# Four gates as two more pairs of seven products, with less fill per retention chunk

## The chip, the core and the metric

The kernel runs on one core of a Trainium2 chip. A core has five engines that work side by side, each on its own queue of instructions: TensorE (PE, matmuls; its weight loads are listed as PEld), VectorE (DVE), ScalarE (ACT), GpSimd (POOL) and SyncE (SP, which here issues most of the DMA loads). POOL issues the stores. Matmul results land in PSUM, in banks of 128 x 512 floats, and DVE and ACT take them from there. The metric is the time of one execution on the device, in microseconds (us); the time given for a kernel is the median of its runs.

## The reference

One layer of an encoder in float32: a half-step feed-forward part, a token mixing, and a second half-step feed-forward part, each between two RMS norms. The sequence has 1024 tokens of width 1024. The change lies in the token mixing:

```python
def _token_mixing(u, w_in, ..., w_ret_out, w_na_out, w_out, pos):
    rq, rk, rv, rg, nq, nk, nv, g_ret, g_na = jnp.split(u @ w_in, points, axis=-1)
    ...
    y = _bidirectional_retention(q, k, heads(rv, RET_V_DIM), decay_fwd, decay_bwd)
    y = y * lax.rsqrt(jnp.mean(y * y, axis=-1, keepdims=True) + RMS_EPS)
    ...
    y_ret = (jax.nn.silu(rg) * y) @ w_ret_out
    y_na = _neighborhood_attention(na_heads(nq), na_heads(nk), na_heads(nv), rel_bias) @ w_na_out
    merged = jax.nn.sigmoid(g_ret) * y_ret + jax.nn.sigmoid(g_na) * y_na
    return merged @ w_out
```

One projection of u gives everything: queries, keys, values and a Silu gate for the retention (4 heads, 128 wide keys, 256 wide values), queries, keys and values for the neighbourhood attention (8 heads of 64), and two gates as wide as the model, `g_ret` and `g_na`. The retention runs over chunks of 128 tokens in both directions. `sigmoid(g_na)` is what the change is about: 1024 columns, eight blocks of 128.

## The kernel before

**Precision.** Every operand is split into a high and a low part (`split`, lines 57 to 66: ACT copies the high part with rounding, DVE subtracts it from the source), and every product is three matmuls, high x high, high x low, low x high (`mm3`, lines 92 to 96).

**Pairs of seven products.** A projection block can be computed in two ways. Directly, as in `gate` (line 1475), one block of 128 output columns over 1024 tokens is 2 halves of the tokens times 8 steps of 128 input columns, each a `mm3` of three 128 x 512 matmuls. Or two blocks together as a `Pairs.run` (line 555), a Winograd form of Strassen's scheme: weights and activations are cut into quarters, and seven products of 4 steps each (12 matmuls) take the place of eight. The activations' factors (a11, a12, a22, s1 to s4) are in SBUF already; the weights' factors are made per pair by DVE, and DVE also adds up the results out of PSUM. The list `jobs` (lines 1400 to 1404) says which blocks go as pairs: four of the neighbourhood's queries and keys, then alternating a pair of the retention's queries and keys (with rotary) and a pair of its Silu gate, and at last two pairs of `g_na`, blocks 0 to 3. Pairs 3, 12 and 13 have their first two products computed earlier, by `leads` at line 1409, and read them back. The loop at line 1434 runs the pairs one after the other; `run` prepares the next pair's weights on the way unless it is told not to (`nxt`, false for pair 3 and the last). What isn't in `jobs` is computed directly.

**Fill.** The neighbourhood attention (`na_cores`, line 929) and the retention (`ret_cores`, line 1120) are made of small matmuls with long chains through DVE and ACT. So that PE has something to do meanwhile, `products` (line 1490) is a generator of independent work, one `mm3` per step, and the two functions call `fill(n)` at fixed places to issue n steps of it. The steps come in a fixed order: 128 for the retention's values (`vproj`) and one that only marks their end, four `g_na` gates (blocks 4 to 7) of 16 steps, four `g_ret` gates of 16, four halves of 8, four halves of 8 with a split of the attention's output between them, and 64 for the neighbourhood's output projection, which multiplies by the `g_na` gates read back from memory (line 1512). That is 385. `NA_FILL` (12, 2, 2) gives 12 steps ahead of the neighbourhood attention and 2 + 2 in each of its 34 rounds, 148 in all. `RET_FILL` has nine numbers, used in `ret_cores` as n[0] to n[8]: ahead of everything (line 1222), at a head's begin (1226), after each of the 7 updates of the backward sweep (1233), before the scores (1239), before the forward chunks (1242), in each of the 8 chunks between the scores and the update (1248), behind the chunk's products (1266), behind the store (1269), and ahead of each store that is left at the very end (1272). What is left of the fill then is drained at line 1536.

**A retention head.** The backward sweep (line 1231) updates the backward state chunk by chunk: three 128 x 256 matmuls (`update`), whose results DVE accumulates (line 1174, tile `sb`). The forward part (line 1243) has, per chunk, the scores of the next chunk, an update of the forward state `st` with its split into `sfh` and `sfl`, the products `cross` (with both states) and `inner`, and a norm, whose result is transposed on PE and multiplied by the Silu gate (`rg`, line 1217) one or two chunks later. In the last chunk the keys of the next head are transposed, scaled and split (`kdec`, tiles `kdh`, `kdl`), and the next head's k, q and v are split (`kl`, `ql`, `vl`). Behind the last head stands the retention's output projection: the gated result is loaded again and split (tile `xy`, line 1545) and multiplied.

**Order.** A planner places the instructions of each engine at build time, by the program's order and by when it reckons their operands ready. Each engine then runs its queue in that order.

Of the kernel before, what the change touches and what calls it, by code (L numbers as in the profile page):

```python
# [13 lines left out]
AF = mybir.ActivationFunctionType  # L14
# [14 lines left out]
NHP = 4  # L29

NA_FILL = (12, 2, 2)
RET_FILL = (14, 2, 2, 4, 2, 3, 0, 1, 2)
FLIP_FILL = (12, 12, 12, 12, 2)
LOADS = (6, 9, 12, 15, 18, 22, 28, 33, 38)
NA_UNITS = ((0, 0, 0), (3, 1, 0), (1, 0, 1), (1, 0, 2), (4, 1, 1), (4, 1, 2), (2, 0, 3), (5, 1, 3))
# [1241 lines left out]
def trunk_layer(ctx: ExitStack, tc, x, xt, g1a, w1i, w1o, g1b, gma, wmt, wnv, wrv, logits, dtab, rope, bias,  # L1277
# [11 lines left out]
    def dt(name, shape):  # L1289
        return dram.tile(shape, F32, name=name)  # L1290
# [3 lines left out]
    d = {  # L1294
        "a21": dt("a21", [P, 4, 512]),
        "nq": dt("nq", [NHP, P, S]), "nk": dt("nk", [NHP, P, S]), "nv": dt("nv", [16, 64, 512]), "nvg": dt("nvg", [4, 4, P, 512]),
        "no": dt("no", [NHP, P, S]), "rq": dt("rq", [RH, P, S]), "rk": dt("rk", [RH, P, S]),
        "rv": dt("rv", [TT, P, D]), "rg": dt("rg", [8, P, S]), "ry": dt("ry", [8, P, S]),
        "dec": dt("dec", [P, 536]), "far": dt("far", [3, 2, P, 512]), "far1": dt("far1", [3, 2, P, 512]), "far2": dt("far2", [3, 2, P, 512]), "sr": dt("sr", [8, P, S]), "sn": dt("sn", [8, P, S]), "z": dt("z", [8, P, S]), "m": dt("m", [8, 2, P, S]),
    }  # L1300
# [6 lines left out]
    def pool(stack, name, side="left"):  # L1307
        return stack.enter_context(tc.tile_pool(name=name, bufs=1, side=side, reuse_waits="tile"))
# [46 lines left out]
    def xh(t, k):  # L1355

        return a21 if (t, k) == (1, 0) else wx.op(("a11", "a12", None, "a22")[2 * t + k])
# [3 lines left out]
    def vproj(src, groups, done):  # L1361

        w = []
        for toks in groups:
            banks = {t: c.bank() for t in toks}
            for k in range(KT):
                if k == len(w):
                    w += ahead.pop(k // 2) if k // 2 in ahead else c.load_w(src[k // 2])
                    if k > 3 and qk:
                        c.after(c.fetch, qk)  # L1370
                        qk.clear()
                for t in toks:
                    tt = slice((t % 4) * P, (t % 4 + 1) * P)
                    c.mm3(banks[t], [q[:, k % 4, tt] for q in xh(t // 4, k // 4)], w[k], k == 0, k == KT - 1)
                    yield
            for t in toks:
                done(t, banks[t])
# [3 lines left out]
    def ev():  # L1381
        return evpool[0].tile([P, S], F32, tag="ev", name="ev", bufs=3)
# [9 lines left out]
    def done_rv(j):  # L1392
        def f(t, b):
            e = ev()
            nc.scalar.copy(e[:, :512], b)
            c.store(d["rv"][t][:, j * 512:(j + 1) * 512], e[:, :512])
        return f


    jobs = [(16 + i, 20 + i, d["nq"][i], d["nk"][i], None) for i in range(NHP)]  # L1400
    for i in range(RH):
        jobs += [(i, 4 + i, d["rq"][i], d["rk"][i], "rotary"),
                 (8 + 2 * i, 9 + 2 * i, d["rg"][2 * i], d["rg"][2 * i + 1], AF.Silu)]
    jobs += [(32 + 2 * i, 33 + 2 * i, d["sn"][2 * i], d["sn"][2 * i + 1], AF.Sigmoid) for i in range(2)]
    mx = Pairs(c, wx, [(wmt[j[0]], wmt[j[1]]) for j in jobs], 3, joined=False)

    def first():
# [67 lines left out]
    def gate(i, dst, halves=(0, 1)):  # L1475

        w = c.load_w(wmt[i])
        e = ev()
        for h in halves:
            hs = slice(h * 512, (h + 1) * 512)  # L1480
            b = c.bank()
            for k in range(KT):
                ks = slice((k % 4) * P, (k % 4 + 1) * P)
                c.mm3(b, [p[:, ks] for p in w[k // 4]], [q[:, k % 4] for q in xh(h, k // 4)], k == 0, k == KT - 1)
                yield
            nc.scalar.activation(e[:, hs], b, AF.Sigmoid)
        hs = slice(halves[0] * 512, halves[-1] * 512 + 512)
        c.store(dst[:, hs], e[:, hs])

    def products():  # L1490
        for j in range(2):
            yield from vproj(wrv[j], ((0, 1, 2), (3, 4, 5), (6, 7)), done_rv(j))
        yield "rv"
        for i in range(4, 8):
            yield from gate(32 + i, d["sn"][i])
        for i in range(4):
            yield from gate(24 + i, d["sr"][i])
        for i in range(4, 8):
            yield from gate(24 + i, d["sr"][i], (1,))
        x1_stack.close()  # L1500
        opool = pool(o_stack, "o", "right")
        oop = [opool.tile([P, 4, S], F32R, name=f"o{q}") for q in "hl"]
        for i in range(4, 8):
            raw = c.raw(d["no"][i - 4])
            c.split(oop[0][:, i - 4], oop[1][:, i - 4], raw)
            yield from gate(24 + i, d["sr"][i], (0,))

        for i in range(8):
            if i % 2 == 0:
                w = c.load_w(wno[i // 2])  # L1510
            e = ev()
            nc.sync.dma_start(e, d["sn"][i])
            for h in range(2):
                hs = slice(h * 512, (h + 1) * 512)
                b = c.bank()
                for k in range(4):
                    c.mm3(b, [p[:, k * P:(k + 1) * P] for p in w[i % 2]], [q[:, k, hs] for q in oop], k == 0, k == 3)
                    yield
                nc.vector.tensor_tensor(e[:, hs], b, e[:, hs], ALU.mult)
            c.store(d["z"][i], e)  # L1520

    fill = Filler(products())
    with tc.tile_pool(name="na", bufs=1, reuse_waits="tile") as na:
        early = []
# [5 lines left out]
    with tc.tile_pool(name="ret", bufs=1, reuse_waits="tile") as ret:  # L1530
        ret_cores(c, ret, mix, d, dec, fill, RET_FILL, early)
    y_stack = ExitStack()
# [175 lines left out]
```

## Time and profile before

| what | us |
|---|---|
| median of 3 runs | 2209.81 |
| lowest and highest run | 2209.61 and 2209.9 |
| the profiled execution, its time | 2210.64 |
| its span, first to last instruction | 2208.9 |
| PE busy in the span | 2186.8 |
| DVE busy | 1574.1 |
| ACT busy | 959.9 |
| POOL busy | 588.7 |

The profile's page is of one execution. An engine's busy time is the union of its instructions' durations; matmuls overlap in it. The granted clock of TensorE was 0.999 of full speed. In the trace the pairs of the mixing run from about 700 to 975 us, the neighbourhood attention from about 975 to 1150, the retention from about 1155 to 1390. L94, L95 and L96 are the three matmuls of `mm3`, L62 and L63 the two instructions of `split`. A name such as `wl<-wraw,wh` is the tile written and the tiles read.

### The profile page before, as it was taken

What the parts mean: (1) busy time and instruction counts of PE and PEld (TensorE: products, weight loads), DVE (VectorE), ACT (ScalarE), POOL (GpSimd) and SP (SyncE); (2) the same over time, 40 slices, a digit from 0 to 9 for tenths busy, and PEclk for the clock granted to TensorE, in tenths of its full rate; (3) what the DMA queues carried; (4) which work ended last, traced back from release to release, by engine and by line L of the source; (5) the groups of instructions that cost most, each with busy time, mean ns of one, the idle gap of its engine ahead of it and who ended that gap; (6) DMA issues with size and microseconds to landing.
All of it is one profiled execution on the core that took longest, in us unless ns stands there. A gap on an engine that the chain in (4) does not pass through costs nothing.

```text
span 2208.9 us, 29722 instructions
## 1 busy us (share of the span) xinstructions
PE 2186.8 (99%) x10232; PEld 1824.4 (83%) x10232; DVE 1574.1 (71%) x2767; ACT 959.9 (43%) x1970; POOL 588.7 (27%) x766
## 2 busy tenths in 40 slices
PE   8999999999999999999999999999999999999998
PEld 7878888888888888888888888888888888888887
DVE  7898887655569757777766677643999787867444
ACT  7444434322345322367775565322544343433232
POOL 2122212169421122311001222101112121216942
PEclk9999999999999999999999999999999999999999
DMA  7354544597745555575543466785446343549865
GB/s 267 129 194 173 200 167 169 220 374 284 246 174 188 197 170 145 146 237 180 184 168 128 145 210 222 272 303 185 156 153 226 130 170 133 181 170 373 276 224 185
DMA packets 151206, 444.63 MB, mean 201 GB/s; under 512 B 19472, under 2 KB 46224, under 8 KB 148944
## 3 DMA queue, kind: packets, MB, share of 16 engines
q1 hardware_dynamic: 107584, 302.97, 40.7%
q0 software_dynamic: 43472, 139.77, 17.6%
q8 instruction: 81, 1.33, 0.2%
q14 instruction: 69, 0.57, 0.1%
HBM read 294.54 MB, written 152.32 MB: 202 GB/s over the span
## 4 chain that ended last, share of the span: by engine, by line
PE 90%; DVE 4%; issue 3%; ACT 1%; DMA 1%; POOL 1%; POOLq 0%; SPq 0%; DVEq 0%; ACTq 0%
PE ps L94 28%; PE ps L95 28%; PE ps L96 28%; PE pt L95 1%; PE pt L94 1%; PE pt L96 1%; PE pt L1002 1%; PE ps L983 1%; DMA g0s<-gth 1%; PE pt L133 0%; DVE wl L63 0%; PE pt L1216 0%; POOL rstd L104 0%; DMA gt<-in_dram 0%; POOL g0a L69 0%
## 5 line engine op out<-in xcount | busy, mean ns | idle before, releaser
L63 DVE TENSOR_TENSOR wl<-wraw,wh 128x512 fp32r<-128x512 f32 x440 | 292.4, 686 | 54.1 <-ACT wh L62 53.3
L62 ACT CAST wh<-wraw 128x512 fp32r<-128x512 f32 x444 | 255.2, 618 | 135.2 <-PE ps L95 57.4
L94 PE MATMUL ps<-wh,g 128*128 128x512 f32 x548 | 214.1, 391 | 0.4 <-DVE tmp L231 0.4
L95 PE MATMUL ps<-wl,g 128*128 128x512 f32 x548 | 213.6, 390 | 0.0
L96 PE MATMUL ps<-wh,g 128*128 128x512 f32 x548 | 213.3, 389 | 0.0
L63 DVE TENSOR_TENSOR wl<-w,wh 128x512 fp32r<-128x512 f32 x77 | 78.8, 1044 | 83.9 <-ACT wh L62 83.7
L63 DVE TENSOR_TENSOR wl<-x,wh 128x512 fp32r<-128x512 f32 x77 | 79.9, 1054 | 76.1 <-ACT wh L62 74.6
L62 ACT CAST wh<-t 128x512 fp32r<-128x512 f32 x58 | 36.1, 622 | 212.2 <-DVE t L575 130.4
L94 PEld LDWEIGHTS ps<-wh,g 128*128 128x128 f32 x548 | 102.9, 188 | 22.0 <-DVE tmp L231 0.7
L95 PEld LDWEIGHTS ps<-wl,g 128*128 128x128 f32 x548 | 102.9, 188 | 21.4 <-DVE wl L63 0.7
L96 PEld LDWEIGHTS ps<-wh,g 128*128 128x128 f32 x548 | 102.9, 188 | 21.3
L94 PE MATMUL ps<-a11h,wh 128*128 128x512 f32 x276 | 108.7, 395 | 1.5 <-ACT a11h L62 1.5
L94 PE MATMUL ps<-a22h,wh 128*128 128x512 f32 x280 | 109.7, 392 | 0.0
L95 PE MATMUL ps<-a11l,wh 128*128 128x512 f32 x276 | 107.9, 391 | 1.3 <-DVE a11l L63 1.3
L95 PE MATMUL ps<-a22l,wh 128*128 128x512 f32 x280 | 109.1, 390 | 0.0
L96 PE MATMUL ps<-a22h,wl 128*128 128x512 f32 x280 | 109.0, 389 | 0.0
L96 PE MATMUL ps<-a11h,wl 128*128 128x512 f32 x276 | 107.7, 390 | 0.9 <-DVE wl L63 0.9
L94 PE MATMUL ps<-a12h,wh 128*128 128x512 f32 x276 | 108.2, 393 | 0.0
L95 PE MATMUL ps<-a12l,wh 128*128 128x512 f32 x276 | 107.5, 390 | 0.0
L96 PE MATMUL ps<-a12h,wl 128*128 128x512 f32 x276 | 107.5, 389 | 0.0
L62 ACT CAST wh<-w 128x512 fp32r<-128x512 f32 x77 | 46.6, 620 | 110.8 <-PE pt L96 54.5
L69 POOL DMA_DIRECT2D g1a<-gth x33 | 17.9, 543 | 285.1 <-ACT gth L672 284.3
(444 smaller groups left out, 6305.5 us busy)
## 6 DMA issues: line engine op xcount, KB each, us to landing
wraw<-in_dram SPq DMA_DIRECT2D x190, 512.0 KB, 4.4
g<-g0s SPq DMA_DIRECT2D x44, 512.0 KB, 4.2
g<-g1s SPq DMA_DIRECT2D x44, 512.0 KB, 4.5
g<-g0a SPq DMA_DIRECT2D x33, 512.0 KB, 4.7
g<-g1a SPq DMA_DIRECT2D x33, 512.0 KB, 4.7
g0s<-gth POOLq DMA_DIRECT2D x44, 256.0 KB, 4.0
g0s<-cmb POOLq DMA_DIRECT2D x44, 256.0 KB, 3.9
g1s<-gth POOLq DMA_DIRECT2D x44, 256.0 KB, 3.9
```

The source lines that it names most:

```text
L62: self.done = [nc.scalar.copy(h, src).ins, (eng or nc.vector).tensor_tensor(l, src, hf, ALU.subtract).ins]
L63: (eng or nc.vector).tensor_tensor(l, src, hf, ALU.subtract).ins]
L69: self.nc.gpsimd.dma_start(dst, src)
L94: mm(ps, a[0], b[0], start=start, stop=False, skip_group_check=again)
L95: mm(ps, a[0], b[1], start=False, stop=False, skip_group_check=again)
L96: self.tail = mm(ps, a[1], b[0], start=False, stop=stop, skip_group_check=again).ins.name
L983: nc.tensor.matmul(bv, q[:, rg * P:(rg + 1) * P], k, start=n == 0, stop=n == 1)
L1002: nc.tensor.transpose(pt[:, j * P:(j + 1) * P], s[:, i % 2, (i // 2) * P:(i // 2 + 1) * P], c.ident)
```

## The change

Blocks 4 to 7 of `g_na` are no longer steps of the fill; the list of jobs gets them as two more pairs, 14 and 15, at its end. They are computed whole, like the Silu pairs, and their sigmoid is taken and stored in the same way as for pairs 12 and 13. The fill is 64 steps shorter, 321 in all. `RET_FILL` asks for one step less after each update of the backward sweep (n[2], 2 to 1) and one less in each forward chunk (n[5], 3 to 2).

```diff
-RET_FILL = (14, 2, 2, 4, 2, 3, 0, 1, 2)
+RET_FILL = (14, 2, 1, 4, 2, 2, 0, 1, 2)
...
-    jobs += [(32 + 2 * i, 33 + 2 * i, d["sn"][2 * i], d["sn"][2 * i + 1], AF.Sigmoid) for i in range(2)]
+    jobs += [(32 + 2 * i, 33 + 2 * i, d["sn"][2 * i], d["sn"][2 * i + 1], AF.Sigmoid) for i in range(4)]
...
         yield "rv"
-        for i in range(4, 8):
-            yield from gate(32 + i, d["sn"][i])
         for i in range(4):
             yield from gate(24 + i, d["sr"][i])
```

## The prediction

> **What bounds the kernel now.** I read the page first: the busy line, the chain that ended last, and the costliest group.
>
> ```profile
> PE 2186.8 (99%) x10232; PEld 1824.4 (83%) x10232; DVE 1574.1 (71%) x2767; ACT 959.9 (43%) x1970; POOL 588.7 (27%) x766
> PE 90%; DVE 4%; issue 3%; ACT 1%; DMA 1%; POOL 1%; POOLq 0%; SPq 0%; DVEq 0%; ACTq 0%
> L94 PE MATMUL ps<-wh,g 128*128 128x512 f32 x548 | 214.1, 391 | 0.4 <-DVE tmp L231 0.4
> ```
>
> TensorE (PE) is busy all the time and owns 90% of the chain. The reader should see one trap: a mean duration of 391 ns is not the price of a matmul, since the durations overlap. The price is the distance between starts. I took it from the timeline of PE at the first product of successive pairs of the mixing, and from a fill step in the retention.
>
> ```profile
> 806.55 0.39 PE L94 MATMUL ps<-a11h,wh 128*128 128x512 f32 x1
> 825.59 0.39 PE L94 MATMUL ps<-a11h,wh 128*128 128x512 f32 x1
> ...
> 844.63 0.39 PE L94 MATMUL ps<-a11h,wh 128*128 128x512 f32 x1
> 865.05 0.39 PE L94 MATMUL ps<-a11h,wh 128*128 128x512 f32 x1
> ...
> 1216.84 0.39 PE L94 MATMUL ps<-a12h,wh 128*128 128x512 f32 x1
> 1217.52 0.39 PE L94 MATMUL ps<-a21h,wh 128*128 128x512 f32 x1
> ```
>
> A pair is 7 products of 12 matmuls, 84 in all; the undisturbed one takes 825.59 - 806.55 = 19.04 us, so a 128x512 matmul costs 0.2267 us. A fill step is three of them, 0.68 us, and the last two rows show just that (1217.52 - 1216.84). The pair from 844.63 took 20.42 us: 1.38 us of waiting.
>
> Next come stretches (the windows view) of the two stages that the change touches, and who PE waits for in them.
>
> ```profile
> 806.55:825.59 19.04, 19.04 (x85) 15.77 (x84) 12.85 (x21) 6.52 (x11) 6.90 (x9) 1.00 0.61 146
> 787.51:941.21 153.70, 152.77 (x673) 125.99 (x672) 108.42 (x172) 45.05 (x80) 46.45 (x66) 1.00 0.61 166
> 1163.30:1389.80 226.50, 225.02 (x1278) 195.62 (x1278) 159.17 (x387) 131.25 (x328) 55.32 (x85) 1.00 0.54 174
> 1218.50:1273.90 55.40, 55.40 (x320) 48.40 (x319) 36.48 (x92) 32.42 (x84) 12.73 (x20) 1.00 0.50 157
> 1273.90:1331.20 57.30, 56.68 (x321) 48.75 (x319) 43.72 (x103) 38.70 (x93) 15.40 (x23) 1.00 0.62 201
> ...
> PE ps L96 <- DVE wl L63: 0.9, 1, 0.9
> ...
> PE ps L95 <- DVE vl L63: 0.8, 1, 0.8
> PE ps L94 <- DVE y L1199: 0.6, 1, 0.6
> ```
>
> The columns are the window, its length, then PE, weight load, DVE, ACT and POOL busy, the clock, the DMA share and the rate. The first row is one pair, the second the eight full pairs of the mixing, the third the retention from its first update, then two of its heads. The waits are the mixing's (740 to 975 us) and the retention's (1150 to 1392 us). So both stages are PE's today, and the retention is so only because the fill sits in it: DVE is at 159.17 of 226.50 us there, 70%.
>
> **The change, part by part.** All sums are against the profiled execution (2210.64 us, span 2208.9); the median of the runs is 2209.81, 0.83 lower, and the forecast is set on the median.
>
> *Products.* A gate of the fill is 2 halves x 8 steps x 3 matmuls = 48; four are 192, 43.5 us. Two pairs are 168, 38.1 us. The difference, 24 x 0.2267 = **-5.4 us**, holds wherever PE does not wait. Trace-reading by the mean would give 24 x 0.39 = 9.4 us. The Trainium skill ("Perfetto Trace Analysis", Identifying the Most-Contended Engine) calls matmul busy time a bad measure because matmuls are pipelined; here the starts, 0.2267 us apart, bear it out.
>
> *Two more pairs in the mixing.* They are ordinary ones, begun and finished in place, as the eight in the second row are. Those average 153.70 / 8 = 19.21 us, 0.17 over the clean pair; DVE has 12.85 us in 19.04. Value **+0.35** for two; bounds 0 and two waits of 1.38, +2.8.
>
> *What moves with them.* Four weight loads, their splits, sigmoids and stores go from the retention to the mixing.
>
> ```profile
> L1486 ACT ACTIVATE ev<-ps x24: 577/590/600, 1138.9 to 1329.2; 128x512 f32<-128x512 f32 x24
> L1450 ACT ACTIVATE ev<-ev x24: 615/632/635, 819.4 to 969.3; 128x512 f32<-128x512 f32 x24
> ```
>
> Eight sigmoids of 0.59 us leave, eight of 0.63 come, on an ACT that has 6.52 us of work in a 19.04 us pair; SP issues four weight loads either way, POOL eight stores for four beside 6.90 of 19.04 us. I cost these at nothing, hidden under PE; without that cover they are inside the +2.8 above.
>
> *Less fill in the retention.* The fill has 385 steps, 148 of them used by the neighbourhood attention before and after alike. The retention asked for 14 + 4 x (2 + 7x2 + 4 + 2 + 8x(3+0+1)) + 4 = 234 of the 237 left; now for 14 + 4 x (2 + 7 + 4 + 2 + 8x(2+0+1)) + 4 = 174, with 173 left. A head loses 15 steps, 10.2 of its 55.4 us. Where a wait was covered, what is late next is shown by the slack of PE's operands. Three places matter.
>
> (a) The last chunk of a head, where DVE also prepares the next head. Rows: when DVE writes the low part of the forward state, and when PE reads it.
>
> ```profile
> 1214.36 0.42 DVE L63 TENSOR_TENSOR sfl<-st,sfh 128x256 fp32r<-128x256 f32 x1
> 1215.69 0.28 PE L95 MATMUL ps<-sfl,qh 128*128 128x256 f32 x1
> 1270.20 0.42 DVE L63 TENSOR_TENSOR sfl<-st,sfh 128x256 fp32r<-128x256 f32 x1
> 1271.10 0.28 PE L95 MATMUL ps<-sfl,qh 128*128 128x256 f32 x1
> 1326.65 0.42 DVE L63 TENSOR_TENSOR sfl<-st,sfh 128x256 fp32r<-128x256 f32 x1
> 1328.08 0.28 PE L95 MATMUL ps<-sfl,qh 128*128 128x256 f32 x1
> ```
>
> Start less end, the slack is 0.91, 0.48 and 1.01 us. A chunk loses one step, 0.68: waits of 0, 0.20 and 0. If the loss of the chunk before is carried along (1.36), they are 0.45, 0.88 and 0.35, together 1.7. Value **+0.9**, between; bounds 0 and 1.7.
>
> (b) The backward sweep: seven updates, each with one step less behind it.
>
> ```profile
> 1218.57:1229.30 10.73, 10.73 (x61) 9.13 (x60) 7.79 (x16) 6.04 (x14) 3.32 (x5) 1.00 0.78 255
> 1323.00:1331.20 8.20, 8.20 (x50) 6.92 (x48) 7.30 (x18) 6.61 (x16) 2.99 (x5) 1.00 0.64 198
> 1337.81 0.68 DVE L63 TENSOR_TENSOR vl<-vl,vh 128x512 fp32r<-128x512 f32 x1
> 1342.34 0.28 PE L95 MATMUL ps<-vl,kdh 128*128 128x256 f32 x1
> ...
> SPq L1211 <- DMA ry<-rg: 79.2, 19, 8.3
> ```
>
> The first row is the sweep of the second head up to its last update: 10.73 us, DVE busy 7.79. Six steps less leave PE 6.65 us, so DVE would be 1.14 us over, 4.6 for four heads. But an update waits for its operands, not for DVE's accumulation behind it; that backlog may drain under the eight steps that lie between the sweep and the first cross product. The operand that comes last, the v of the last head, has 3.85 us of slack (third and fourth row) and six steps take 4.08; its load stands in SP's queue behind loads of rg, which waited 79.2 us for stores to land (last row, 1160 to 1392 us), and DMA does not get faster. Value **+1.1**, a quarter of the excess, as most of it is deferred; bounds 0 and 4.6.
>
> (c) The end of the retention, where eight steps (1+2+2+3) lie behind the last chunk; now there are four, for the fill runs out. The next product needs the first operand of the output projection.
>
> ```profile
> 1386.65 3.88 ACT L62 CAST xy<-wraw 128x1024 fp32r<-128x1024 f32 x4
> 1387.90 0.42 DVE L1217 TENSOR_TENSOR rg<-pt,rg 128x256 f32<-128x256 f32 x1 [0.22 <-PE pt L1216]
> 1388.24 1.22 DVE L63 TENSOR_TENSOR xy<-wraw,xy 128x1024 fp32r<-128x1024 f32 x1
> 1389.78 0.61 PE L94 MATMUL ps<-xy,wh 128*128 128x512 f32 x2
> ```
>
> The split ends at 1389.46, PE reads at 1389.78: 0.32 us of slack, against 2.72 of fill gone, so at most +2.4. The transposes ahead of L1217 move up with PE, the cast is done near 1387.7, so the split could end near 1388.9, while PE would be free near 1387.1 with one product that needs the high part alone (0.23). Value **+1.7**; bounds 0 (if the planner puts the split earlier) and 2.4.
>
> *In between*, in the steady chunks, I add nothing, as the same two rows show there:
>
> ```profile
> 1253.90 0.42 DVE L63 TENSOR_TENSOR sfl<-st,sfh 128x256 fp32r<-128x256 f32 x1
> 1257.47 0.28 PE L95 MATMUL ps<-sfl,qh 128*128 128x256 f32 x1
> ```
>
> The slack is 3.15 us and a chunk loses 0.68. The two waits that PE has today (0.8 + 0.6) may go or move: value 0, bound -1.4.
>
> Sum: -5.44 + 0.35 + 0.9 + 1.1 + 1.7 = **-1.4 us**, 2209.2 for the profiled execution and **2208.4** on the median. Ends: -5.4 - 1.4 = -6.8 (2203.0), and -5.4 + 2.8 + 1.7 + 4.6 + 2.4 = +6.1 (2215.9).
>
> **The rivals.** About 0.2%, 4.4 us, is what a measurement of this kernel can tell from no change.
>
> *All of it arrives.* The planner orders the work anew around the thinner fill, the split at the end comes early, and the slack elsewhere holds: -5.4 to -4.5, 2204.4 to 2205.3. For it: PE's waits in the retention are 1.4 us in 226 today, and the state's slack is mostly over two steps. Against it: (c) has 0.32 us. Chance 0.23.
>
> *DVE and ACT take over the retention.* The same six chunks in the third head and in the last:
>
> ```profile
> 1293.60:1323.00 29.40, 28.78 (x172) 25.10 (x171) 22.41 (x59) 19.52 (x53) 7.49 (x12) 1.00 0.59 194
> 1350.90:1379.00 28.10, 28.10 (x173) 25.04 (x172) 21.54 (x59) 15.55 (x45) 8.15 (x13) 1.00 0.60 192
> ```
>
> Eight splits of the gates leave DVE (some 0.68 each); 153.7 us stay for 226.5 - 43.5 = 183 us of PE, 84%. Each chunk's work goes back and forth between the two engines, and a late instruction holds what stands behind it in its queue. The third head, DVE at 76%, already takes 1.3 us longer than the last for the same chunks, 4.6%. If that is the rule in 183 us, it is 8.4; with (c) and the mixing 2214.8, slower. It decides from 9.8 us of waiting. Against it: the last head has the same DVE load, 77%, and no wait. The Trainium skill ("TensorE: Matmul & The Clock Gate", Architectural detail) has these queues as strictly first in, first out, which speaks for this rival; the trace's order of casts ahead of a state does not contradict it. Chance 0.20.
>
> *The pairs don't run at PE's pace.* Both take 20.42 us like the one from 844.63, or wait for a store: +2.4 more than my value, 2210.8. It is within the forecast's range; its chance, 0.05, is counted there.
>
> **How the numbers follow.** My forecast, within 0.2%: 0.57, its own range 2205.4 to 2213. Faster: 0.23, the first rival. Slower: 0.20, the second. The range of 2203.5 to 2216 takes in both and the ends of the unknown terms, leaving some 0.15 out.
>
> **What would show it.** The pairs: two more 19.0 to 19.2 us periods, PE's wait in the mixing still near 1 us. The retention: from first update to last product about 187 us, with waits on DVE's state and v splits of a few tenths per head; waits of over 2 us a head would mean the second rival. The end: a PE gap of 1 to 2.4 us ahead of the first product with xy; none there means the planner moved the split. The forecast is wrong if PE's waits in the retention sum to under 1 us or over 10.

## The result, and the profile after

| | before | after |
|---|---|---|
| median of 6 runs | 2209.71 | 2220.11 |
| lowest and highest run | 2208.85 to 2210.29 | 2217.32 to 2221.87 |
| profiled execution, its time and span | 2210.64, 2208.9 | 2221.57, 2219.7 |
| first update to first product with xy | 227.28 | 198.91 |

The change costs 10.4 us: ratio 1.0045, interval 1.0035 to 1.0055. The forecast was 2208.4, with a range up to 2216: wrong in sign and out of its range. First the page of after, with its busy line, its chain and its costliest group.

```profile
PE 2188.5 (99%) x10208; PEld 1823.1 (82%) x10208; DVE 1590.5 (72%) x2795; ACT 964.4 (43%) x1978; POOL 587.9 (26%) x770
PE 83%; DVE 6%; issue 5%; ACT 2%; DMA 2%; POOL 1%; SPq 0%; POOLq 0%; DVEq 0%; ACTq 0%
L94 PE MATMUL ps<-wh,g 128*128 128x512 f32 x548 | 214.2, 391 | 0.4 <-DVE tmp L231 0.4
```

PE has 24 matmuls less and is still "99% busy", with more busy time than before. Only the chain tells: PE's share fell from 90 to 83%. Where the time went is read from stretches. The new pairs are the last two of the mixing; here is the timeline of PE at their first products and at the product behind them:

```profile
967.65 0.39 PE L94 MATMUL ps<-a11h,wh 128*128 128x512 f32 x1
...
986.69 0.39 PE L94 MATMUL ps<-a11h,wh 128*128 128x512 f32 x1
...
1005.73 0.39 PE L94 MATMUL ps<-wh,a11h 128*128 128x512 f32 x1
```

Each takes 19.04 us, no wait at all. Now the windows view (columns as in the prediction) of the retention, from its first update to the first product with xy, after and then before:

```profile
1199.91:1398.82 198.91, 187.64 (x1090) 161.48 (x1088) 151.53 (x381) 119.58 (x311) 52.81 (x81) 0.99 0.54 178
```

```profile
1162.50:1389.78 227.28, 225.80 (x1283) 196.00 (x1282) 159.97 (x388) 131.58 (x329) 55.32 (x85) 1.00 0.54 175
```

Four gates of fill, 43.5 us, have left, so 183.8 us were due. It is 198.9: **15.1 us too long**. PE's idle time grew by 9.8 of them, to 11.3 (198.91 - 187.64; before 1.5). The other 5.3 count as busy: a stretch at a lower clock, which the 0.99 hints at, and the first part of each gap, over which the matmul ahead of it, 0.39 us long by its row, still reaches. The account of the span: the first update comes 37.4 us later (1199.91 - 1162.50), the retention is 28.4 shorter, and what follows it is 1.8 longer (2219.7 - 1398.82 against 2208.9 - 1389.78). That gives 10.8, the difference of the spans.

PE's waits of after, between 1150 and 1412 us (total, times, longest):

```profile
PE ps L94 <- DVE y L1199: 4.0, 5, 1.9
PE pt L1216 <- ACT yn L1205: 2.1, 2, 1.7
PE ps L94 <- DVE a L1187: 1.9, 1, 1.9
PE ps L95 <- DVE vl L63: 1.5, 2, 1.0
PE ps L94 <- ACT sfh L62: 0.7, 2, 0.4
PE ps L94 <- ACT xy L62: 0.5, 1, 0.5
PE ps L94 <- ACT y L1197: 0.3, 1, 0.3
```

The costliest releaser is none whose slack the prediction measured. L1199 writes `y`, which no matmul reads; the matmuls that wait for it write `cross` or `inner`. So they wait for the PSUM bank that L1199 still has to read. Three places show what makes these instructions late. The first is one chunk of the third head: SP, ACT, DVE and PE by the timeline.

```profile
1323.41 0.32 SPq L1510 DMA_DIRECT2D ev<-sn  x1
1323.83 0.39 SPq L1148 DMA_DIRECT2D vl<-rv  x1
...
1327.68 0.62 ACT L62 CAST vh<-vl 128x512 fp32r<-128x512 f32 x1 [2.04 <-DMA vl<-rv]
1328.21 0.47 ACT L1197 ACTIVATE y<-ps,dec 128x256 f32<-128x256 f32 x1
...
1328.94 0.48 DVE L1199 SCALAR_TENSOR_TENSOR y<-ps,dec,y 128x256 f32<-128x256 f32 x1
...
1327.33 0.28 PE L96 MATMUL ps<-vh,kdl 128*128 128x256 f32 x1
1329.47 0.39 PE L94 MATMUL ps<-sbh,qh 128*128 128x256 f32 x1 [1.87 <-DVE y L1199]
```

Read it from the last row back. PE waits for L1199, that for ACT's L1197, and that stands in ACT's queue behind a cast of the next chunk's v, whose load landed 3.8 us after its issue. The load in turn was issued behind `ev<-sn` on SP, which had to wait for a store. The second place is the scores of a chunk in the second head:

```profile
1257.08 3.41 SPq L1211 DMA_DIRECT2D rg<-rg  x2
1260.59 0.42 SPq L73 DMA_DIRECT2D wraw<-in_dram  x1
...
1264.58 0.62 ACT L62 CAST wh<-wraw 128x512 fp32r<-128x512 f32 x1 [4.49 <-DMA wraw<-in_dram]
...
1265.23 0.69 DVE L63 TENSOR_TENSOR wl<-wraw,wh 128x512 fp32r<-128x512 f32 x1 [4.81 <-ACT wh L62]
1265.84 0.28 DVE L1187 TENSOR_TENSOR a<-ps,dec 128x128 f32<-128x128 f32 x1
...
1266.18 0.35 PE L94 MATMUL ps<-qh,kh 128*128 128x128 f32 x1 [1.85 <-DVE a L1187]
```

Two loads of rg hold SP until a store has landed; the fill's weights behind them come late, their cast holds ACT, their split holds DVE, and the scores' result, which only had to be taken out of PSUM, waits behind the split. The third is the end:

```profile
1395.87 0.42 ACT L1202 ACTIVATE yn<-y 128x256 f32<-128x256 f32 x1 [0.49 <-DVE y L1200]
...
1397.33 0.51 ACT L1205 ACTIVATE yn<-y,rstd 128x256 f32<-128x256 f32 x1 [0.94 <-POOL rstd L104]
...
1395.82 0.40 PE L96 MATMUL ps<-oh,wl 128*128 128x512 f32 x1
1397.89 0.44 PE L1216 MATMUL pt<-ident,yn 128*128 128x128 f32 x2 [1.67 <-ACT yn L1205]
1398.82 2.41 PE L94 MATMUL ps<-xy,wh 128*128 128x512 f32 x6 [0.50 <-ACT xy L62]
1401.03 0.63 PE L95 MATMUL ps<-xy,wh 128*128 128x512 f32 x1
1401.46 0.63 PE L96 MATMUL ps<-xy,wl 128*128 128x512 f32 x1
```

The fill has run out, and PE waits for the last chunk's norm (ACT, DVE, POOL, ACT), then for ACT's cast of xy. The last two rows show one thing more: starts 0.43 us apart in place of 0.23. The windows view has the granted clock at half speed for 3.4 us behind this gap and behind the one at 1266:

```profile
1266.30:1269.70 3.40, 3.40 (x11) 2.82 (x12) 2.41 (x7) 2.82 (x9) 0.79 (x2) 0.51 0.29 40
1399.50:1402.90 3.40, 3.40 (x10) 2.66 (x9) 3.40 (x4) 2.11 (x3) 0.65 (x1) 0.50 0.98 305
```

Half speed for 3.4 us loses 1.7 us, each time. The second is the 1.8 us behind the retention in the account. Both belong to this execution: the traces of e1, e3 and e10 below have the same gap at the end (1.82 to 1.85 + 0.74 us) with a clock of 1.00 behind it.

### The profile page after: what moved, and what is told of

Its sections match the earlier page's. It is cut to its first block, busy times and chain, and to the rows that moved or that the text cites. A ratio compares the mean times of both kernels' runs of the same rounds, so it can differ in the third digit from the quotient of the medians.

```text
span 2219.7 us, 29752 instructions
## 1 busy us (share of the span) xinstructions
PE 2188.5 (99%) x10208; PEld 1823.1 (82%) x10208; DVE 1590.5 (72%) x2795; ACT 964.4 (43%) x1978; POOL 587.9 (26%) x770
## 4 chain that ended last, share of the span: by engine, by line
PE 83%; DVE 6%; issue 5%; ACT 2%; DMA 2%; POOL 1%; SPq 0%; POOLq 0%; DVEq 0%; ACTq 0%
PE ps L94 26%; PE ps L95 26%; PE ps L96 26%; PE pt L96 1%; PE pt L95 1%; PE pt L94 1%; POOL rstd L104 1%; DVE wl L63 1%; DMA vl<-rv 1%; PE pt L1002 1%; PE ps L983 1%; DMA no<-ot 0%; PE pt L133 0%; ACT s L988 0%; DMA gt<-in_dram 0%
## 5 line engine op out<-in xcount | busy, mean ns | idle before, releaser
L63 DVE TENSOR_TENSOR wl<-w,wh 128x512 fp32r<-128x512 f32 x77 | 79.2, 1048 | 83.4 <-ACT wh L62 83.2
L94 PE MATMUL ps<-s2h,wh 128*128 128x512 f32 x240 | 93.7, 391 | 1.2 <-ACT wh L62 1.2
```

The lines of the kernel that those rows point to most:

```text
L63: (eng or nc.vector).tensor_tensor(l, src, hf, ALU.subtract).ins]
L94: mm(ps, a[0], b[0], start=start, stop=False, skip_group_check=again)
```

## The experiments

Times are medians; each ratio is to the kernel before, run on the same chip. "Waits" are distances between PE's starts beyond the usual one, of over 0.22 us, summed over the retention: 2.0 us before, 14.8 after.

**The loads of rg (e1, e2, e3).** The longest line of SP's waits between 1185 and 1420 us was the store of one chunk's result, for which the load of a later one's gate waits; the second row is the wait of `ev<-sn` from the first place:

```profile
SPq L1211 <- DMA ry<-rg: 88.9, 22, 9.6
...
SPq L1510 <- DMA sr<-ev: 6.6, 2, 6.0
```

e1 and e2 leave the loads out, in after and in before, and multiply by the decay table instead; the Silu gate is not applied.

```diff
-        e = nc.sync.dma_start(rg, d["rg"][2 * h:2 * h + 2, :, cs].rearrange("k p t -> p k t")).ins
...
-        nc.vector.tensor_tensor(rg, pt[:, :256].rearrange("p (k t) -> p k t", k=2), rg, ALU.mult)
+        nc.vector.tensor_tensor(rg, pt[:, :256].rearrange("p (k t) -> p k t", k=2), dec.dm[:, 0:2], ALU.mult)
```

> The changed kernel without the loads of rg (32 of 128 KB): the transposed result is multiplied by a table that lies in SBUF, so the Silu gate is left out; store, DVE work and PE work stay. Theory A (loads of v and of fill weights come late because they stand in SP's queue behind rg loads that wait for the landing of ry stores; a late load holds ACT's cast and what is behind it): the 88.9 us of waits of L1211 go, PE's waits in the retention fall from 11.2 us to under 5, and the time from 2220 to 2209-2214. Theory B (DVE and ACT have too much work and too long chains for the shorter heads, whatever the loads do): PE's waits stay above 8 us and the time at 2216 or more.

> The same edit in the kernel before (the Silu gate is left out): the control. Both theories: PE waits only 1.4 us in the retention there, so 2208-2210, within 2 us of the 2209.7 of before. If it gains more than 3 us, the edit itself takes work away and the gain of the first run must be set against it.

e1: 2217.27, 1.0031 (1.0022 to 1.0041). e2: 2209.91, 0.9997 (0.9988 to 1.0007). By the medians the loads cost 2.8 us in after, though its interval overlaps that of after, and nothing in before, where PE has fill to go on with. Waits for y L1199 stay (3.7 against 4.0): the range of theory B. e3 keeps the loads and orders each behind its own chunk's norm:

```diff
-        if h == 0:
-            c.after(e, early)
+        c.after(e, [sq])
```

> The changed kernel with each load of rg ordered by the planner behind the square of the norm that it belongs to, two chunks ahead of its use, in place of as early as its buffer is reckoned free. Theory A: the waits of L1211 fall under 40 us, PE's waits fall by a third or more, 2212-2217. Theory B: 2218 or more, PE's waits as before.

2219.41, 1.0041 (1.0026 to 1.0056): SP no longer waits for `ry`, yet the time is within the spread of after. A part, then, and not the main one.

**Fill kept for the end (e4).** `RET_FILL` asks for 3 in place of 4 ahead of the scores' start, so four steps more are left at the end.

```diff
-RET_FILL = (14, 2, 1, 4, 2, 2, 0, 1, 2)
+RET_FILL = (14, 2, 1, 3, 2, 2, 0, 1, 2)
```

> The changed kernel with one fill step less ahead of each head's first scores (n[3] from 4 to 3), so that four steps are left for the end. Both theories: PE's gap at the end (1.8 and 0.7 us, then some 2 us at half the clock) shrinks by up to 2.7 us, so 2216-2219 if the four heads don't mind; 2220 or more if the step ahead of the scores was needed too.

2215.97, 1.0026 (1.0016 to 1.0036), 4.1 us less than after. In the profiled executions the gap at the end falls from 2.57 to 1.09 us, and the half-speed stretch behind it goes, 3.2 us together; but e1, e3 and e10 lack that stretch with the gap still there, so its 1.7 us can't be put down to the four steps. The waits within moved too (y L1199 5.3), since any edit gives the planner a new order.

**Half of the change (e5, e6).** One pair moved, with one of the two thinnings each: e5 keeps 2 steps per backward update and thins the forward chunks, e6 the other way round.

```diff
-RET_FILL = (14, 2, 1, 4, 2, 2, 0, 1, 2)
+RET_FILL = (14, 2, 2, 4, 2, 2, 0, 1, 2)
...
-    jobs += [(32 + 2 * i, 33 + 2 * i, d["sn"][2 * i], d["sn"][2 * i + 1], AF.Sigmoid) for i in range(4)]
+    jobs += [(32 + 2 * i, 33 + 2 * i, d["sn"][2 * i], d["sn"][2 * i + 1], AF.Sigmoid) for i in range(3)]
...
+        for i in range(6, 8):
+            yield from gate(32 + i, d["sn"][i])
```

> Half the change: one pair moved instead of two (blocks 4 and 5; 6 and 7 stay in the fill), and only the forward chunks thinned (RET_FILL 14, 2, 2, 4, 2, 2, 0, 1, 2). PE has 2.7 us less to do than before. Theory F (the forward chunks are where the vector engines fall behind, and PE waits for the PSUM bank that y L1199 still reads): PE's waits in the chunks stay at 4 us or more, 2211-2216. Theory W (the backward sweep and the loads of v and weights around it): few waits, 2206-2209.

> The other half: one pair moved, only the backward sweep thinned (RET_FILL 14, 2, 1, 4, 2, 3, 0, 1, 2). PE has 2.7 us less to do. Theory F: the chunks are as before, so 2206-2209 with waits of 1 to 3 us. Theory W: 2211-2216.

e5: 2221.69, 1.005 (1.0036 to 1.0065). e6: 2217.48, 1.0035 (1.0022 to 1.0048). Not additive: each half costs most of the whole, 11.5 and 7.2 us over before, and both lie above what either theory expected. Half of e6's 7.9 us of waits are one of 3.7 us, and its timeline shows the first place again, longer:

```profile
1323.50 6.40 SPq L1512 DMA_DIRECT2D ev<-sn  x3
...
1330.95 0.42 SPq L1148 DMA_DIRECT2D vl<-rv  x1
...
1337.42 0.62 ACT L62 CAST vh<-vl 128x512 fp32r<-128x512 f32 x1 [4.49 <-DMA vl<-rv]
```

The loads `ev<-sn` of the neighbourhood's projection wait for stores too, and the v of the retention is late behind them. The longest wait of e5, 3.4 us, also follows a cast of v that waited 3.72 us for its load.

**One bank less (e7).** The forward update and the inner product share a bank, so that `cross` waits less for L1199.

```diff
-                update(h, 0, kf, cc, v, old, st)
+                both = c.bank()
+                update(h, 0, kf, cc, v, old, st, both[:, 256:])
...
-            cross, inner = c.bank(), c.bank()[:, :256]
+            cross, inner = c.bank(), (both if cc < NC - 1 else c.bank())[:, :256]
```

> The changed kernel with the forward update and the inner product of a chunk in the two halves of one PSUM bank, so that a chunk takes three banks and the fill's, not four and the fill's. Theory F with the bank as the link: the waits on y L1199 (4.0 us) go to under 1.5 and the half-clock stretches get fewer, 2212-2217. If DVE and ACT are late whatever the banks do, PE waits for the state or the scores instead (sfl, al) and the time stays at 2218-2221.

```profile
PE ps L94 <- DVE st L1174: 6.9, 10, 2.1
```

2223.85, 1.0062 (1.0047 to 1.0077). Worse, by a wait that the edit brought in: `inner` now waits until L1174 has read the other half of its bank. It tells nothing of the banks themselves.

**Density (e8, e9).** e8 moves both pairs but keeps the old `RET_FILL`, so the fill is gone before the last head. e9 is the kernel before with the thin `RET_FILL` alone, no gate moved.

```diff
-RET_FILL = (14, 2, 2, 4, 2, 3, 0, 1, 2)
+RET_FILL = (14, 2, 1, 4, 2, 2, 0, 1, 2)
```

> The two pairs moved, but RET_FILL as before the change: the heads are as dense as before until the fill is used up, in the last head, which then has none. Every theory that blames the thinning: PE waits in the first two heads as before (under 2 us in all), and all the loss in the last head and the end; 2220-2235 in all. If the first two heads show waits of 2 us and more each, it isn't the thinning but the new order of the work.

> The kernel before with RET_FILL alone changed (14, 2, 1, 4, 2, 2, 0, 1, 2): no gate moves, PE has as much to do as before, and the 60 steps that the heads no longer ask for (most of the neighbourhood's output projection) run at the end, where they also cover the last norm. Theory N (the thinner heads alone make DVE and ACT late, whatever the fill is): PE's waits are some 8 to 12 us over all heads, 2217-2223. Theory K (what is left as fill is the dear kind: in the first heads there are now as many cheap gates, 16 steps per weight load, as before, and the loads of the output projection, ev from sn, no longer stand ahead of v in SP's queue): waits of under 1 us in the first two heads, 2209-2214.

e8: 2233.51, 1.0106 (1.0086 to 1.0127). e9: 2225.42, 1.007 (1.0055 to 1.0085). Its window, from first update to first product with xy, what is left of the fill included, and the first of its waits:

```profile
1162.06:1402.37 240.31, 230.67 (x1283) 196.37 (x1282) 167.58 (x396) 135.91 (x335) 54.35 (x85) 1.00 0.56 180
```

```profile
PE ps L94 <- DVE y L1199: 2.8, 7, 0.8
PE pt L1216 <- ACT yn L1205: 2.0, 3, 1.0
PE ps L94 <- ACT y L1197: 1.7, 3, 1.3
```

The same 1283 matmuls as before take 13.0 us longer, 240.31 against 227.28, because the same fill is spread thinner and the rest comes behind it. So **the thinning alone costs such a time, with no gate moved**. It is not the whole story, as PE's waits by head show (the last column runs on to the first product with xy):

| PE's waits, us | first head | second | third | last |
|---|---|---|---|---|
| before | 1.0 | 0 | 0.7 | 0.3 |
| after | 2.4 | 5.6 | 3.0 | 3.8 |
| e8 | 0.8 | 7.1 | 0.6 | 14.0 |
| e9 | 2.0 | 2.1 | 2.8 | 6.4 |

The last head of e8 has no fill, and there most of its 22.5 us lie. But its second head is as dense as before and waits 7.1 us, which its expectation took for a sign against the thinning as the only cause. The longest of these waits, 2.2 us, is the first place once more: three loads `ev<-sn` take 6.7 us to issue on SP, and ACT then waits 3.99 us for the v behind them. With 64 steps moved away the later kinds of fill come into earlier heads; the second head of after, too, waits 3.5 us more than that of e9 at the same density. How much of the loss is the thinning and how much is which fill lies in which head, no run parts.

**Is it only an unlucky order? (e13, e14).** Two other spreads of the old density in the kernel before:

```diff
-RET_FILL = (14, 2, 2, 4, 2, 3, 0, 1, 2)
+RET_FILL = (14, 2, 2, 4, 2, 2, 1, 1, 2)
```

(e14 has 14, 3, 2, 3, 2, 3, 0, 1, 2.)

> The kernel before with as many fill steps per chunk, one of them behind the products of the chunk and not ahead of its update (RET_FILL 14, 2, 2, 4, 2, 2, 1, 1, 2). Theory N (density): within 2 us of before, 2208-2212, waits of PE under 4 us in the retention. Theory L (a lucky order): 2215 or more, waits of 8 us and more as in the thinned kernels.

> The kernel before with one fill step per head moved from ahead of the scores to the head's begin (RET_FILL 14, 3, 2, 3, 2, 3, 0, 1, 2). Theory N: 2208-2212. Theory L: 2215 or more.

2212.39, 1.0008 (0.9999 to 1.0018), and 2210.11, 0.9999 (0.9989 to 1.0008). Against before on the same chip that is +1.9 and -0.35 us. These two new orders alone are worth no more than some 2 us; 10 is more than that.

**Both loads late (e10, e11, e12).** rg as in e3, and the loads of `sn` behind the last product issued:

```diff
-            nc.sync.dma_start(e, d["sn"][i])
+            c.after(nc.sync.dma_start(e, d["sn"][i]).ins, [c.tail])
```

> The changed kernel with both kinds of loads that wait for a store (rg for ry, ev for sr or z) placed by the planner at their place in the program and not as early as a buffer is reckoned free. If loads of v that stand behind them in SP's queue make the two long waits (2.03 and 1.19 us, and the half-clock stretch behind): both go under 0.5, 2213-2217. If not, 2218 or more.

> The same with the four steps kept for the end as well (n[3] from 4 to 3): the end's gap of 2.6 us falls under 1.2 and with it a half-clock stretch; 1.5 to 4 us less than the run without it, 2210-2215. 2216 or more if the heads need that step.

> Control for the two runs with late loads: the same two placements (rg and ev loads at their place in the program) in the kernel before. If late loads matter only where the heads are thin: 2208.5-2210.5. If they are a gain by themselves, as large as in the changed kernel (4 us): 2205-2207.

e10 is after with both: 2216.26, 1.003 (1.002 to 1.004), 3.9 us less than after. The 2.01 us wait of the second place is gone, the 2.03 us of the first is 0.62, and no stretch in the retention is at half speed; but the wait for v in the last head's sweep, expected to go too, grew from 1.19 to 1.59. e11 adds e4's tail: 2212.89, 1.0014 (1.0005 to 1.0024), 3.4 less again. e12 is before with the late loads: 2209.64, 0.9996 (0.9987 to 1.0006), nothing gained: in before these loads cost nothing where they were.

**The norm's chain (e16, e18).** What is left in e11, 8.5 us of waits, was put down to the work of ACT and DVE behind each chunk. e16 is e11 without the norm's square, root and scaling; the normalisation of the retention is left out.

```diff
-        nc.vector.tensor_tensor(y, inner, y, ALU.add)
-        ss = c.small.tile([P, 2], F32, tag="ss", name="ss", bufs=4)
-        sq = nc.scalar.activation(yn, y, AF.Square, scale=1.0 / 16.0, accum_out=ss[:, 0:1]).ins
-        nc.vector.tensor_scalar(ss[:, 1:2], ss[:, 0:1], EPS, None, ALU.add)
-        r = c.rstd(ss[:, 1:2], 1)
-        nc.scalar.activation(yn, y, AF.Copy, scale=r[:, 0:1])
+        sq = nc.vector.tensor_tensor(yn, inner, y, ALU.add).ins
```

> The run with late loads and the kept end (e11, 2212.9) without the second half of the norm: square, mean, reciprocal root and scaling of each retention chunk are left out (two ACT instructions and a read of the accumulator, one small DVE instruction, one POOL instruction per chunk; PE's work and all loads stay). If the waits that remain come from the work of ACT and DVE per chunk: PE's waits in the retention fall from 8.5 us to under 4, 2206-2210. If they come from the loads or from the order alone: 2211-2214.

2238.02, 1.0125 (1.0108 to 1.0142): a miss by 25 us, though the waits fell to 3.5. Most products of the kernel, from its first stage to its last, were slower: by the median up to 0.232 us between the starts of 128x512 matmuls, against 0.227 in e18, while a few kinds, those with xy among them, kept 0.227. A pair of the mixing, long before any norm, in e16 and then in e18, which differs from it in one line (the small tile is still allocated, unused):

```profile
817.14 0.40 PE L94 MATMUL ps<-a11h,wh 128*128 128x512 f32 x1
836.44 0.40 PE L94 MATMUL ps<-a11h,wh 128*128 128x512 f32 x1
```

```profile
806.04 0.39 PE L94 MATMUL ps<-a11h,wh 128*128 128x512 f32 x1
825.08 0.39 PE L94 MATMUL ps<-a11h,wh 128*128 128x512 f32 x1
```

```diff
+        c.small.tile([P, 2], F32, tag="ss", name="ss", bufs=4)
         sq = nc.vector.tensor_tensor(yn, inner, y, ALU.add).ins
```

> The same as e16 (the norm's square, root and scaling in the retention left out, the two loads late, tail 3), but the small tile ss, 32 bytes a partition, is still allocated although nothing uses it, so that every later tile stands where it stood in e11. Layout theory (e16's slower matmuls come only from the shifted tiles): matmul starts 227 ns apart again, first update near 1199 us, PE's waits in the retention about 3.5 us as in e16 instead of 8.5, time 2207 to 2209. Rival (the loss of e16 comes from the left-out work itself, by another order of instructions): starts still 231 ns apart, 2236 to 2239. If the pitch is back and the waits are 8 us again, 2212 to 2213: then the work of DVE and ACT behind each chunk is not what holds PE.

19.30 us in e16, 19.04 in e18; e18 takes **2206.2, 0.9982 (0.9973 to 0.9992)**. So e16's loss came from the place of its tiles in SBUF. With the layout kept, leaving out the norm is worth 6.7 us against e11. The retention's window in e11 and in e18:

```profile
1199.10:1389.93 190.83, 183.97 (x1090) 160.11 (x1089) 151.00 (x380) 120.20 (x312) 52.72 (x81) 1.00 0.58 189
```

```profile
1200.10:1385.07 184.97, 181.74 (x1090) 159.81 (x1089) 148.44 (x347) 96.93 (x217) 32.39 (x49) 1.00 0.61 195
```

184.97 us, near the 183.8 that were due. DVE's share of it is 80% (148.44 of 184.97), in e11 79%: so it isn't DVE's load that held PE. What left is 23 us of ACT and a chain over three engines. ACT waited in that chain, with all that stands in its queue behind; e11 between 1185 and 1395 us:

```profile
ACT yn L1202 <- DVE y L1200: 20.1, 18, 1.5
ACT yn L1205 <- POOL rstd L104: 19.0, 27, 1.1
```

These runs don't part ACT's 23 us of work from its 39 us of waiting. PE's waits in e18:

```profile
PE ps L94 <- DVE y L1199: 2.7, 3, 1.0
PE ps L95 <- DVE vl L63: 0.4, 1, 0.4
```

In e11 these were 3.0 and 0.7, with 1.6 for yn and 1.3 for L1197 besides: the norm's removal took the latter two, and left nearly all of the first.

**Better spreads (e15, e17).** e11 with 14, 3, 1, 2, 2, 2, 0, 1, 2, and with 14, 2, 1, 3, 2, 1, 1, 1, 2:

> The changed kernel with late loads and RET_FILL 14, 3, 1, 2, 2, 2, 0, 1, 2: one more step at a head's begin, where the last run waited 1.55 us, taken from ahead of the scores; four steps stay for the end. If that wait goes and nothing else comes: 2210-2212. If the shorter stretch ahead of the scores makes new waits: 2213-2216.

> The same as e11 with one fill step per chunk moved from ahead of the update to behind the products (RET_FILL 14, 2, 1, 3, 2, 1, 1, 1, 2), so that two steps in place of one lie between a chunk's products and the next ones' first bank. If the bank that y L1199 reads is late by a few tenths at that place: 2209-2212. If the step was needed ahead of the update: 2213-2217.

2212.53, 1.0011 (1.0001 to 1.002), and 2211.98, 1.0008 (0.9998 to 1.0017). e17 is the best form of the change that computes all of it, and no better than before: **no version beat the kernel before** with the whole computation.

## Why the prediction was wrong

- **Products, -5.44.** Right as a sum: 10208 matmuls in place of 10232, and pairs at 19.04 us. e9 less after is 5.3 by the medians, which fits but proves little: the two also differ in where PE waits, 13.2 and 14.8 us in all.
- **The two pairs, +0.35 (0 to 2.8).** Their periods are 19.04 and 19.04: 0. That weights, sigmoids and stores cost nothing there was right.
- **(a) Last chunk of a head, +0.9.** Right in place: PE sat idle 0.7 us for sfh (before none of that size) and 0.2 for sfl, in the last chunks of the first two heads. By the distances between starts, which is what it cost, these are 1.8, at the upper bound of 1.7.
- **(b) Backward sweep, +1.1.** Right in size: the waits for vl rose from 0.8 to 1.5 (by the starts from 1.0 to 1.9), one of 1.0 in the last head's sweep, on the operand it named. The excess of DVE that the number was taken from is not seen in the other sweeps, so the size is in part luck.
- **(c) The end, +1.7 (0 to 2.4).** Mis-sized (its own figures, 1388.9 - 1387.1 - 0.23, give 1.6). It said that the transposes move up with PE and only the split is late. The transposes themselves waited, 1.67 us idle, for the last chunk's norm, whose chain over ACT, DVE and POOL it did not count; with ACT's cast of xy 2.57, and in the profiled execution 1.7 more for the half clock: 4.3.
- **"In between, in the steady chunks, I add nothing".** The step that failed. By the distances between starts the waits grew by 12.8 us, and 7.5 of these are neither (a), (b) nor the end: they lie where the sum has 0. It read 3.15 us of slack on one operand in one chunk, the state's low part, and took that for the chunk's. But PE also waits for a bank until L1199 has read it, and for the scores' drain: 4.0 and 1.9 us, and 1.7 of half clock behind the latter. These instructions are late because they stand in order behind others: on ACT and DVE behind casts and splits whose loads wait in SP's queue for stores (e10: 3.9 us), and behind the norm's chain (e18: 6.7, the last of the end's gap among it).
- **The rows that misled.** SP's 79.2 us for rg were quoted and used only for (b), and before they were harmless indeed (e2, e12): the fill covered them. A wait that costs nothing under a thick cover is no evidence for the cost under a thin one.
- **The rivals.** The second had the sign and the mechanism in kind (a late instruction holds what stands behind it), and its point of decision, 9.8 us of waiting: it was 15.8, 10.4 + 5.4 by the medians. Its measure was wrong: it argued from DVE's share, which e18 leaves at 80% while the time falls. At 0.20 it was rated too low, as the two waits it had in hand (1.4 us) already had L1199 as one of their releasers. The first rival fell.

Three things stay open. Medians of e10, e11 and e18 take off 3.9 + 3.4 + 6.7 = 14.0 us, but each edit reorders the rest, so the parts are good to some 2 us (e13), and the intervals of after and e10, and of e10 and e11, overlap a little; those of after and e11, and of e11 and e18, don't. And the 2.7 us for L1199 in e18 stand behind casts of v on ACT that wait for their loads in two of the three places by its timeline; no run removed those. And e8's second head shows that thinning is not the only way to these waits.

## What to carry to other kernels

Fill that hides chains is not worth its matmuls alone: before it is thinned, ask for every instruction on which PE can wait, the readers of its PSUM banks too, what stands ahead of it in its engine's queue, and not what slack one operand has. Under thin fill, loads that must wait for a store belong behind those that need not, on the same queue (3.9 us here; in the kernel before, e12, it changed nothing). And run the thinning alone: e9 takes one line, and shows at once what it costs.

## What the runs showed of the hardware

Behind a gap of some 2 us on PE the granted clock was halved in some cases and not in others. In after, gaps of 2.01 us (at 1266) and of 1.83 + 0.74 us (at the end) were each followed by 3.4 us at half clock; the 2.03 us gap at 1329 was not, nor the one at the end in e1, e3 and e10, nor the 3.71 us one in e6, where the clock shows 1.00 in both 3.4 us windows behind it:

```profile
1338.00:1341.40 3.40, 1.59 (x9) 1.44 (x10) 3.19 (x7) 2.33 (x7) 0.72 (x1) 1.00 0.61 162
1341.40:1344.80 3.40, 3.40 (x21) 2.91 (x20) 3.30 (x8) 3.07 (x8) 1.30 (x2) 1.00 0.43 158
```

The Trainium skill ("TensorE: Matmul & The Clock Gate", Part 1: The HAM clock gate) has the clock fall after at least one idle window of about 3.4 us, in windows that run freely. The length of the slow stretch agrees with the trace; the gap that sets it off was shorter here, and whether it does seems to hang on where it falls.

And 32 bytes per partition of an unused tile (8 bytes in four buffers) are worth 31.8 us here, e16 against e18: the matmuls of the pair shown start 0.2298 us apart (19.30 / 84) in place of 0.2267. Which tiles must not share which addresses, the runs don't tell.
